# One 64-partition product in place of two 128-partition products when a norm's roots are spread to all partitions

## The chip, the cores and the metric

The kernel runs on one core of one Trainium2 chip. The metric is the device time of one execution in microseconds (us), the median of several runs. The engines of the core are named as the profile names them: PE (TensorE, products) with PEld (its weight loads), DVE (VectorE), ACT (ScalarE), POOL (GpSimd) and SP (SyncE, which issues most transfers). SBUF is the on-chip memory of 128 partitions, PSUM the memory that TensorE writes.

## The reference

A two-layer decoder trunk on one sequence of 512 tokens with 1024 features. What matters here is that each block begins with an RMSNorm, so that a root of a mean square over the features is wanted for every token, and that the product with the weights comes after it:

```python
def rmsnorm(x, g):
    xf = x.astype(jnp.float32)
    y = xf * lax.rsqrt(jnp.mean(xf * xf, axis=-1, keepdims=True) + EPS)
    return (y * g.astype(jnp.float32)).astype(x.dtype)
...
    for i in range(DEPTH):
        xn = rmsnorm(h, norm_mix[i])
        if i < N_A_LAYERS:
            a = i
            h = h + mixer_a(xn, a_w_in[a], a_norm_v[a], a_w_s[a], a_b_s[a], a_w_out[a])
        else:
            b = i - N_A_LAYERS
            h = h + mixer_b(xn, b_w_q[b], b_sinks[b], b_w_o[b], kblk, vblk)
        h = h + conv_ffn(rmsnorm(h, norm_ffn[i]), f_w_up[i], f_conv_w[i], f_conv_b[i], f_w_down[i])
        h = h + per_layer_embed(h, p[i], norm_ple[i], ple_w_in[i], ple_w_gate[i], ple_b_gate[i])
        if i == N_A_LAYERS - 1:
            kblk, vblk = shared_kv(h, norm_kv, w_kv)
    return rmsnorm(h, norm_final)
```

## The kernel before

**Layout.** The residual stream `h` lies with features on partitions: 8 tiles of 128 features x 512 tokens. Every weight is read once, in pieces of up to 1 MB (`load`, issued on SP in a fixed order), and cut into a high and a low half in the reduced type fp32r: `pump` copies the raw piece to `wh` on ScalarE (L163) and subtracts to get `wl` on VectorE (L164), one unit of 128 x 1024 at a time, with four units ahead of the one being multiplied. The activations are split likewise, and `mm3` (L190 to L192) or `mm3t` (L201 to L203) form a product as high x high + low x high + high x low.

**The norm.** Because the root is one number per token, it is not needed before the product with the weights: the product of the unnormalized, gain-scaled `h` is formed, and its result is multiplied by the root of each token. `Norm` does this. `take` or `square` squares each tile of `h` and adds the squares up in `acc` (128 x 512). `turn` transposes `acc` in blocks of 32 x 32 on VectorE and reduces each block, which leaves `quarter`: on 128 partitions, 16 numbers each. `begin` multiplies `quarter` by `alike`, which is four 128 x 32 blocks of stacked identities over D: the result `ps` (128 x 16 in PSUM) has the mean square of token 32 b + t on partition 32 a + t in column b, the same for each a from 0 to 3. `inv_root` then adds EPS on VectorE (L329) and raises to -1/2 on POOL (L331).

Before the change `begin` picks the columns so that `rt` is 128 x 4: token 128 c + p on partition p in column c (four small operations on VectorE, one for each quarter of the partitions). `rstd` turns it into a 128 x 512 tile, in which every partition holds the roots of all 512 tokens along the free axis: `spread` splits `rt` into `rh` and `rl`, multiplies the identity by each (two operations of 128 x 512 on VectorE, L344), sums over the partitions by two products with a 128 x 128 tile of ones (L347), and ScalarE copies the result out of PSUM (L320).

**Who uses which.** There are six norms of this class. In program order: n0 (ahead of the first mixer), nf0 (ahead of the first feed-forward block), np0 (first per-layer embedding), n1 (the shared keys and values, and the queries), nf1 and np1 (the same blocks in the second layer). In `ffn` (nf0, nf1) and `ple` (np0) `begin` stands behind the first 24 products of a chunk and `rstd` behind the next 24. Only `rstd` is used there. In n0, n1 and np1 the row form `rt` is used as well, where tokens lie on partitions: as the scale of the Gelu of n0 (L558), for the values of n1 (L711, L712 and `nrt`, L685), and for the last two blocks of 128 tokens in np1 (L998, L1001).

For n0, `begin` stands behind the products of the first half of the second column block of the mixer's `v` branch; 48 products follow ahead of `rstd`. ScalarE then goes through Gelu and squares of all eight `v` tiles, which ends in `sv` and a second root `vrt`; VectorE multiplies `zv` by it (L567), and PE reads `zv` in the products `s` (L584) behind the 48 products of the first chunk of `u`. For n1, `begin` stands behind the key products and `rstd` behind 24 query products. For np1, `begin` stands ahead of the last 24 products of 256 columns of the first four gate tiles, and eight transposes of `h` (L945) follow before `rstd`.

**Order.** The order of instructions on each engine is decided by a scheduler from program order, priorities and data; each engine then works through its own list in that order. An instruction that waits holds everything behind it on its engine.

Of the kernel before, what the change touches and what calls it, by code (L numbers as in the profile page):

```python
# [8 lines left out]
F32 = mybir.dt.float32  # L9
F32R = mybir.dt.float32r  # L10
AF = mybir.ActivationFunctionType
ALU = mybir.AluOpType

P = 128
D = 1024
S = 512
KD = D // P
NC = S // P
# [30 lines left out]
def tile_yoco(ctx: ExitStack, tc: tile.TileContext, t, out: bass.AP, out_b: bass.AP):  # L49
    nc = tc.nc  # L50

    const = ctx.enter_context(tc.tile_pool(name="const", bufs=1))
# [8 lines left out]
    def psum(name):  # L61
        return mmp.tile([P, S], F32, tag="mm", name=name)
# [178 lines left out]
                         start=True, stop=True)  # L241
    mean = const.tile([P, 1], F32, name="mean")
    nc.vector.memset(mean, 1.0 / D)
    minus_half = const.tile([P, NC], F32, name="minus_half")
    nc.vector.memset(minus_half, -0.5)
    ident = const.tile([P, P], F32, name="ident")
    make_identity(nc, ident)
# [2 lines left out]
    for q in range(4):  # L250
        s = slice(32 * q, 32 * (q + 1))
        nc.vector.tensor_scalar_mul(alike[s], ident[s, s].rearrange("p (o t) -> p o t", o=1).to_broadcast([32, 4, 32]),
                                    1.0 / D)


    def split_scaled(src, g, hi, lo):
# [15 lines left out]
    class Norm:  # L272
# [30 lines left out]
            nc.vector.tensor_reduce(self.quarter, sq.rearrange("p (b f) -> p b f", f=32),  # L303
                                    axis=mybir.AxisListType.X, op=ALU.add)

        def begin(self):

            if self.quarter is None:
                self.turn()
            ps = psum(f"{self.name}ms")[:, : S // 32]  # L310
            nc.tensor.matmul(ps, alike.rearrange("p a b -> p (a b)"), self.quarter, start=True, stop=True)
            ms = ps.rearrange("p (c r) -> p r c", r=4)
            self.rt = inv_root([(slice(32 * r, 32 * (r + 1)), ms[32 * r : 32 * (r + 1), r, :]) for r in range(4)],
                               self.name, n=NC)
            return self.rt

        def rstd(self):

            r = tp.tile([P, S], F32, tag="rstd", name=f"{self.name}rstd")
            nc.scalar.copy(r, spread(self.rt, NC, self.name))  # L320
            return r

    def inv_root(ms, name, scale=1.0, n=None):
        if n is None:
            n = ms.shape[1]
            ms = [(slice(None), ms)]
        m = const.tile([P, n], F32, tag=f"ms{n}", bufs=2, name=f"{name}m")
        for some, x in ms:
            nc.vector.tensor_scalar(m[some, :], x, scale, EPS, op0=ALU.mult, op1=ALU.add)  # L329
        r = const.tile([P, n], F32, tag=f"rt{n}", bufs=2, name=f"{name}rt")  # L330
        nc.gpsimd.tensor_tensor(r, m, minus_half[:, :n], op=ALU.pow)  # L331
        return r

    def spread(r, n, name):

        dh = tp.tile([P, n, P], F32R, tag="acc", name=f"{name}dh")
        dl = tp.tile([P, n, P], F32R, tag="acc", name=f"{name}dl")
        ps = psum(f"{name}sp")[:, : n * P]
        rh = const.tile([P, n], F32R, tag=f"rh{n}", bufs=1, name=f"{name}rh")
        nc.vector.tensor_copy(rh, r)  # L340
        rl = const.tile([P, n], F32, tag=f"rl{n}", bufs=1, name=f"{name}rl")
        nc.vector.tensor_sub(rl, r, rh.bitcast(F32))
        for d, x in ((dh, rh.bitcast(F32)), (dl, rl)):
            nc.vector.tensor_mul(d, ident.rearrange("p (o t) -> p o t", o=1).to_broadcast([P, n, P]),  # L344
                                 x.rearrange("p (c o) -> p c o", o=1).to_broadcast([P, n, P]))
        for d, st, en in ((dh, True, False), (dl, False, True)):
            nc.tensor.matmul(ps, ones, d.rearrange("p a b -> p (a b)"), start=st, stop=en)  # L347
        return ps
# [19 lines left out]
    def ffn(l, norm, nxt):  # L368

        xs = norm.xs[0][0]  # L370
        rstds = []

        def up(j):
            parts = chunk(256, KD)
            pss, cs = [], []
            for s in range(2):
                ps = psum(f"up{j}_{s}")
                mm3(ps, parts, xs, s * P)
                pss.append(ps)
                if j == 0:  # L380
                    rstds.append((norm.begin, norm.rstd)[s]())
            for s, ps in enumerate(pss):
                hs = tp.tile([P, S], F32, tag="hs", name=f"hs{j}_{s}")
                nc.vector.tensor_mul(hs, ps, rstds[1])  # L384
                col = s * NJ + j
                cw = [v("conv_w", (l * 3 + i) * 2 * NJ + col) for i in range(3)]
                c = tp.tile([P, S], F32, tag=f"c{s}", name=f"c{j}_{s}")
                nc.scalar.activation(c, hs, AF.Identity, bias=v("conv_b", l * 2 * NJ + col), scale=cw[2])  # L388
                nc.vector.scalar_tensor_tensor(c[:, 1:], hs[:, : S - 1], cw[1], c[:, 1:], op0=ALU.mult, op1=ALU.add)  # L389
                nc.vector.scalar_tensor_tensor(c[:, 2:], hs[:, : S - 2], cw[0], c[:, 2:], op0=ALU.mult, op1=ALU.add)  # L390
                cs.append(c)
            a = tp.tile([P, S], F32, tag="sg", name=f"a{j}")
            nc.scalar.activation(a, cs[0], AF.Silu)
            nc.vector.tensor_mul(a, a, cs[1])  # L394
            hi = ap.tile([P, S], F32R, tag=f"ah{j % SLOTS}", name=f"ah{j}")
            lo = ap.tile([P, S], F32R, tag=f"al{j % SLOTS}", name=f"al{j}")
            split(a, hi, lo)
            return hi, lo

        act = [up(0)]  # L400
        pe = None
        for i, (j0, j1) in enumerate(PARTS):
            act += [up(j) for j in range(j0 + 1, j1)]
            last = j1 == NJ
            if last:
                pe = ple_in_both() if l else ple_in(l)
            nact = [] if last else [up(j1)]
            dense_add(act, j1 - j0, nxt if last else None)
            act = nact
        return pe  # L410
# [44 lines left out]
    def ple(l, norm, nxt, pe):  # L455
        xs = norm.xs[0][0]
        rstd, held = None, []
        for c in range(4):
            parts = chunk(256, KD)
            for j in range(2):  # L460
                ps = psum(f"gate{c}_{j}")
                mm3(ps, parts, xs, j * P)
                held.append((2 * c + j, ps))
                if c == 0:
                    rstd = (norm.begin, norm.rstd)[j]()
                if c or j:
                    for m, ps in held:
                        z = tp.tile([P, S], F32, tag="hs", name=f"z{m}")
                        nc.vector.tensor_mul(z, ps, rstd)
                        sg = tp.tile([P, S], F32, tag="sg", name=f"gs{m}")  # L470
                        nc.scalar.activation(sg, z, AF.Sigmoid, bias=v("ple_b_gate", l * KD + m))
                        nc.vector.tensor_mul(sg, sg, pe[m])
                        nc.vector.tensor_add(h[m], h[m], sg)
                        nxt.take(m)
                    held = []
# [645 lines left out]
```

## Time and profile before

| | us |
|---|---|
| median of 3 runs | 1136.89 (1136.75 to 1136.90) |
| the profiled execution | 1136.71 |
| its span on the core | 1134.8 |
| PE busy | 1125.2 |
| DVE busy | 756.0 |
| ACT busy | 517.1 |
| POOL busy | 103.6 |

Rows of the timeline begin with the start in us from the start of the span and the duration in us; then come engine, line of the kernel, operation, output <- inputs, shapes and how many were merged. In square brackets stands how long the engine was idle before, and what ended that. A product's row on PE is longer than the time until the next one starts, because products are pipelined. Rows of groups end with the busy sum, the mean of one in ns, and the idle time ahead of the group with what ended it.

### The profile page before, as it was taken

What the parts mean: (1) busy time and instruction counts of PE and PEld (TensorE: products, weight loads), DVE (VectorE), ACT (ScalarE), POOL (GpSimd) and SP (SyncE); (2) the same over time, 40 slices, a digit from 0 to 9 for tenths busy, and PEclk for the clock granted to TensorE, in tenths of its full rate; (3) what the DMA queues carried; (4) which work ended last, traced back from release to release, by engine and by line L of the source; (5) the groups of instructions that cost most, each with busy time, mean ns of one, the idle gap of its engine ahead of it and who ended that gap; (6) DMA issues with size and microseconds to landing.
All of it is one profiled execution on the core that took longest, in us unless ns stands there. A gap on an engine that the chain in (4) does not pass through costs nothing.

```text
span 1134.8 us, 13579 instructions
## 1 busy us (share of the span) xinstructions
PE 1125.2 (99%) x5266; PEld 940.6 (83%) x5266; DVE 756.0 (67%) x1166; ACT 517.1 (46%) x827; POOL 103.6 (9%) x169
## 2 busy tenths in 40 slices
PE   9999999999999999999999999999999999999997
PEld 7888888888888888888888887888888888888896
DVE  7366477763677357557888997777636763675675
ACT  6533444441344234544656775444323442445562
POOL 2000200000000000021204451000000000000212
PEclk9999999999999999999999999999999999999999
DMA  8422323223232322333124323323223233224302
GB/s 300 140 88 75 111 75 111 86 100 112 75 102 92 101 95 89 109 105 107 69 81 130 82 87 126 135 75 111 94 92 111 66 102 111 93 88 154 112 1 75
DMA packets 25775, 115.40 MB, mean 102 GB/s; under 512 B 2920, under 2 KB 8176, under 8 KB 16240
## 3 DMA queue, kind: packets, MB, share of 16 engines
q1 hardware_dynamic: 25152, 113.89, 29.9%
q8 instruction: 41, 0.67, 0.3%
q10 hardware_dynamic: 560, 0.66, 0.2%
q14 instruction: 22, 0.18, 0.1%
HBM read 108.24 MB, written 2.11 MB: 97 GB/s over the span
## 4 chain that ended last, share of the span: by engine, by line
PE 94%; DVE 3%; issue 1%; DMA 1%; ACT 0%; POOL 0%; SPq 0%; POOLq 0%; DVEq 0%
PE up L190 14%; PE up L191 14%; PE up L192 14%; PE d L192 8%; PE d L190 8%; PE d L191 8%; PE gate L190 2%; PE gate L191 2%; PE gate L192 2%; PE u L191 1%; PE u L190 1%; PE u L192 1%; PE o L191 1%; PE o L192 1%; PE o L190 1%
## 5 line engine op out<-in xcount | busy, mean ns | idle before, releaser
L163 ACT CAST wh<-wraw 128x1024 fp32r<-128x1024 f32 (+2 forms) x197 | 202.0, 1028 | 265.0 <-PE d L191 131.3
L164 DVE TENSOR_TENSOR wl<-wraw,wh 128x1024 fp32r<-128x1024 f32 (+1 forms) x198 | 239.1, 1209 | 122.0 <-ACT wh L163 121.6
L190 PE MATMUL up<-nf00h,wh 128*128 128x512 f32 x352 | 137.1, 390 | 0.0
L190 PE MATMUL up<-nf10h,wh 128*128 128x512 f32 x352 | 137.0, 389 | 0.0
L191 PE MATMUL up<-nf00l,wh 128*128 128x512 f32 x352 | 136.9, 389 | 0.0
L192 PE MATMUL up<-nf00h,wl 128*128 128x512 f32 x352 | 136.9, 389 | 0.0
L191 PE MATMUL up<-nf10l,wh 128*128 128x512 f32 x352 | 136.9, 389 | 0.0
L192 PE MATMUL up<-nf10h,wl 128*128 128x512 f32 x352 | 136.9, 389 | 0.0
L190 PE MATMUL d<-ah,wh 128*128 128x512 f32 x352 | 136.9, 389 | 0.0
L191 PE MATMUL d<-al,wh 128*128 128x512 f32 x352 | 136.9, 389 | 0.0
L192 PE MATMUL d<-ah,wl 128*128 128x512 f32 x352 | 136.9, 389 | 0.0
L388 ACT ACTIVATE c<-hs,vec 128x512 f32<-128x512 f32 x88 | 71.5, 815 | 72.0 <-DVE hs L384 71.2
L389 DVE SCALAR_TENSOR_TENSOR c<-hs,vec,c 128x511 f32<-128x511 f32 x88 | 65.8, 749 | 34.5 <-ACT c L388 34.4
L364 DVE TENSOR_TENSOR h<-h,d 128x512 f32<-128x512 f32 x56 | 38.4, 686 | 74.0 <-PE d L192 74.0
L190 PEld LDWEIGHTS up<-nf00h,wh 128*128 128x128 f32 x352 | 66.1, 188 | 13.8
L191 PEld LDWEIGHTS up<-nf10l,wh 128*128 128x128 f32 x352 | 66.1, 188 | 13.8
L191 PEld LDWEIGHTS d<-al,wh 128*128 128x128 f32 x352 | 66.1, 188 | 13.7
L190 PEld LDWEIGHTS d<-ah,wh 128*128 128x128 f32 x352 | 66.1, 188 | 13.8
L192 PEld LDWEIGHTS up<-nf10h,wl 128*128 128x128 f32 x352 | 66.1, 188 | 13.7
L192 PEld LDWEIGHTS d<-ah,wl 128*128 128x128 f32 x352 | 66.1, 188 | 13.7
L192 PEld LDWEIGHTS up<-nf00h,wl 128*128 128x128 f32 x352 | 66.1, 188 | 13.7
L261 ACT CAST ah<-a 128x512 fp32r<-128x512 f32 x44 | 27.4, 622 | 109.7 <-DVE a L394 109.6
(453 smaller groups left out, 2050.1 us busy)
## 6 DMA issues: line engine op xcount, KB each, us to landing
wraw<-in_w_up SPq DMA_DIRECT2D x44, 1024.0 KB, 4.8
wraw<-in_w_down SPq DMA_DIRECT2D x16, 896.0 KB, 4.6
wraw<-in_w_down SPq DMA_DIRECT2D x8, 1024.0 KB, 4.9
wraw<-in_w_gate SPq DMA_DIRECT2D x8, 1024.0 KB, 4.8
wraw<-in_w_u SPq DMA_DIRECT2D x4, 1024.0 KB, 6.3
wraw<-in_w_out SPq DMA_DIRECT2D x4, 1024.0 KB, 4.8
wraw<-in_w_q SPq DMA_DIRECT2D x4, 1024.0 KB, 5.0
wraw<-in_w_o SPq DMA_DIRECT2D x4, 1024.0 KB, 4.9
```

The costliest lines, as they stand in the source:

```text
L163: nc.scalar.copy(hi, src)
L164: nc.vector.tensor_sub(low, src, hi.bitcast(F32))
L190: nc.tensor.matmul(ps, wh[:, a:b], xh, start=st, stop=False)
L191: nc.tensor.matmul(ps, wh[:, a:b], xl, start=False, stop=False)
L192: nc.tensor.matmul(ps, wl[:, a:b], xh, start=False, stop=en)
L261: nc.scalar.copy(hi, src)
L364: nc.vector.tensor_add(h[m], h[m], ps)
L388: nc.scalar.activation(c, hs, AF.Identity, bias=v("conv_b", l * 2 * NJ + col), scale=cw[2])
L389: nc.vector.scalar_tensor_tensor(c[:, 1:], hs[:, : S - 1], cw[1], c[:, 1:], op0=ALU.mult, op1=ALU.add)
```

## The change

`begin` now takes the mean squares of all 512 tokens from the first 64 partitions of `ps` as they lie there (64 x 16, so each token twice), and forms the root of all of them in one go on POOL. On all 64 partitions it rounds them to fp32r into `hl`; on partitions 32 to 63 it overwrites that with what the rounding lost. `rstd` multiplies `pick`, two stacked 32 x 32 identities, by `hl` (one operation of 64 x 512 on VectorE) and sums over the 64 partitions by one product with 64 rows of ones: the high halves on 32 of the partitions and the low halves on the others add up in the product itself. The row form `rt` is made as before, behind it, and only where it is used (`rows`); `ffn` and `ple` ask for none. `spread` stays for the final norm.

```diff
-    minus_half = const.tile([P, NC], F32, name="minus_half")
+    minus_half = const.tile([P, S // 32], F32, name="minus_half")
...
+    pick = const.tile([64, 32], F32, name="pick")
+    for q in range(2):
+        s = slice(32 * q, 32 * (q + 1))
+        nc.vector.tensor_copy(pick[s], ident[s, s])
...
-        def begin(self):
+        def begin(self, rows=True):
...
-            ps = psum(f"{self.name}ms")[:, : S // 32]
+            n = S // 32
+            ps = psum(f"{self.name}ms")[:, :n]
             nc.tensor.matmul(ps, alike.rearrange("p a b -> p (a b)"), self.quarter, start=True, stop=True)
-            ms = ps.rearrange("p (c r) -> p r c", r=4)
-            self.rt = inv_root([(slice(32 * r, 32 * (r + 1)), ms[32 * r : 32 * (r + 1), r, :]) for r in range(4)],
-                               self.name, n=NC)
-            return self.rt
+            r = inv_root([(slice(None), ps[:64])], f"{self.name}s", n=n, parts=64)
+
+            self.hl = const.tile([64, n], F32R, tag="hl", bufs=1, name=f"{self.name}hl")
+            nc.vector.tensor_copy(self.hl, r)
+            low = slice(32, 64)
+            nc.vector.tensor_sub(self.hl[low], r[low], self.hl[low].bitcast(F32))
+            if rows:
+                ms = ps.rearrange("p (c r) -> p r c", r=4)
+                self.rt = inv_root([(slice(32 * r, 32 * (r + 1)), ms[32 * r : 32 * (r + 1), r, :]) for r in range(4)],
+                                   self.name, n=NC)
+                return self.rt
...
+            n = S // 32
+            d = tp.tile([64, n, 32], F32R, tag="acc", name=f"{self.name}d")
+            nc.vector.tensor_mul(d, pick.rearrange("p (o t) -> p o t", o=1).to_broadcast([64, n, 32]),
+                                 self.hl.bitcast(F32).rearrange("p (c o) -> p c o", o=1).to_broadcast([64, n, 32]))
+            ps = psum(f"{self.name}sp")
+            nc.tensor.matmul(ps, ones[:64], d.rearrange("p a b -> p (a b)"), start=True, stop=True)
             r = tp.tile([P, S], F32, tag="rstd", name=f"{self.name}rstd")
-            nc.scalar.copy(r, spread(self.rt, NC, self.name))
+            nc.scalar.copy(r, ps)
...
-    def inv_root(ms, name, scale=1.0, n=None):
+    def inv_root(ms, name, scale=1.0, n=None, parts=P):
...
-                    rstds.append((norm.begin, norm.rstd)[s]())
+                    rstds.append(norm.rstd() if s else norm.begin(rows=False))
...
-                    rstd = (norm.begin, norm.rstd)[j]()
+                    rstd = norm.rstd() if j else norm.begin(rows=False)
```

In the order that the scheduler gives to VectorE, the instructions of a norm with rows are: the wide addition of EPS, two of the four narrow ones, the rounding copy (which waits for POOL), a narrow one, the subtraction, a narrow one, then `d`; at n1 a weight split (L164) stands ahead of `d`, and at n0 one stands behind it. `nrt` comes behind `d`. The two copies of `pick` stand right behind the four of `alike`. PE's order is the same but for the product that is gone; on ScalarE and VectorE the order of a few neighbours differs in both feed-forward blocks and in np0's block.

More of the change, by code (lines that the diff above doesn't have):

```diff
@@ L326, in inv_root @@
             ms = [(slice(None), ms)]
-        m = const.tile([P, n], F32, tag=f"ms{n}", bufs=2, name=f"{name}m")
+        m = const.tile([parts, n], F32, tag=f"ms{n}", bufs=1 if parts < P else 2, name=f"{name}m")
         for some, x in ms:
             nc.vector.tensor_scalar(m[some, :], x, scale, EPS, op0=ALU.mult, op1=ALU.add)
-        r = const.tile([P, n], F32, tag=f"rt{n}", bufs=2, name=f"{name}rt")
-        nc.gpsimd.tensor_tensor(r, m, minus_half[:, :n], op=ALU.pow)
+        r = const.tile([parts, n], F32, tag=f"rt{n}", bufs=1 if parts < P else 2, name=f"{name}rt")
+        nc.gpsimd.tensor_tensor(r, m, minus_half[:parts, :n], op=ALU.pow)
         return r
```

## The prediction

> **What bounds the kernel now.** I read the page first: its busy shares and its chain of waits.
>
> ```profile
> span 1134.8 us, 13579 instructions
> PE 1125.2 (99%) x5266; PEld 940.6 (83%) x5266; DVE 756.0 (67%) x1166; ACT 517.1 (46%) x827; POOL 103.6 (9%) x169
> PE 94%; DVE 3%; issue 1%; DMA 1%; ACT 0%; POOL 0%; SPq 0%; POOLq 0%; DVEq 0%
> ```
>
> TensorE is busy for 99% and carries 94% of the chain, so a product taken away is worth its spacing, and whatever makes PE wait costs its full length. The view of waits, for PE alone, says how rare that is today:
>
> ```profile
> PE o L191 <- POOL ol L867: 0.8, 1, 0.8
> PE v L203 <- DVE wl L164: 0.4, 1, 0.4
> ```
>
> None of the six norms makes PE wait for its root now. So the question at each is whether the new way of making `d` still ends before PE reaches the spread product, and what a second root behind it delays.
>
> **The products removed.** Each norm's two spread products become one. The timeline of PE at nf0 (columns here and below: start and duration in us):
>
> ```profile
> 156.46 0.40 PE L347 MATMUL nf0sp<-nf0dh,ones 128*128 128x512 f32 x1
> 156.69 0.39 PE L347 MATMUL nf0sp<-nf0dl,ones 128*128 128x512 f32 x1
> 156.93 0.39 PE L190 MATMUL up<-nf00h,wh 128*128 128x512 f32 x1
> ```
>
> Starts are 0.23 us apart though a row lasts 0.39. Half the partitions do not shorten the streaming of 512 columns, so one product is saved, not one and a half: 6 x 0.23 = -1.38 us.
>
> **A product on 64 rows.** No row shows one. The only shape other than 128\*128 in the trace is the 128\*8 pair:
>
> ```profile
> 145.09 0.38 PE L605 MATMUL turned<-ident,vec 128*8 128x128 f32 x2
> ...
> 145.54 0.40 PE L191 MATMUL up<-nf00l,wh 128*128 128x512 f32 x1
> ```
>
> From 145.09 to 145.54 stream 2 x 128 + 512 columns, 1.5 times 0.23 = 0.34 us at the usual pace; 0.11 more were spent. I take 0.11 for each change of shape and back, since that is the nearest row: 6 x 0.11 = +0.66. Below, it is 0. Above, both ends of the odd product lie bare: a row lasts 0.39 and the next starts after 0.23, so 0.16 of tail is hidden, twice that is 0.32; and if weight loads can't run ahead either, 0.19 more each:
>
> ```profile
> L190 PEld LDWEIGHTS up<-nf00h,wh 128*128 128x128 f32 x352 | 66.1, 188 | 13.8
> ```
>
> so 0.70 a norm, 4.2 in all. The Trainium skill, TensorEngine Tiling (Array Packing), section Tiling Modes, says that a change of the tiling mode, 64 rows against 128 among them, drains the array; by it the sum would hold the two bare tails instead of my 0.11. That is rival B. No run here shows it yet.
>
> **The root on POOL.** It grows from 128x4 to 64x16, so from 4 elements a partition to 16. Groups of POOL by shape:
>
> ```profile
> L331 POOL TENSOR_TENSOR n1rt<-n1m,minus_half 128x4 f32<-128x4 f32 x1 | 1.0, 1018 | 10.5 <-DVE n1m L329 10.5
> L331 POOL TENSOR_TENSOR fin0rt<-fin0m,minus_half 128x2 f32<-128x2 f32 x1 | 0.7, 708 | 1.5 <-DVE fin0m L329 1.5
> L331 POOL TENSOR_TENSOR fin1rt<-fin1m,minus_half 128x1 f32<-128x1 f32 x1 | 0.5, 547 | 0.0
> ```
>
> 1, 2 and 4 columns take 547, 708 and 1018 ns: 155 to 161 a column. Sixteen: 1018 + 12 x 155 = 2878 ns, 1.86 more than now. Partitions need not help, as they work side by side. Below: 1.02, if width were free; above: four times 1.02, 4.07. I take 2.88, as three rows lie on one line.
>
> **Norms without rows (nf0, np0, nf1).**
>
> ```profile
> 151.09 0.67 DVE L329 TENSOR_SCALAR nf0m<-nf0ms 32x4 f32<-32x4 f32 x4 [0.93 <-PE nf0ms L311]
> ...
> 153.78 0.68 DVE L344 TENSOR_TENSOR nf0dl<-ident,nf0rl 128x512 fp32r<-128x512 f32 x1
> ```
>
> One tensor_scalar (0.67 / 4, about 0.16) stands for four, then 0.08 until POOL starts, 2.88, 0.04 back, two small operations (about 0.4 with their dependence) and one multiplication of 0.68: `d` is ready at 151.09 + 4.25 = 155.3. PE needs it at 156.46, so 1.1 us are to spare and PE's own 24 products hide it. DVE stands still during the root, but the weight split behind it is read by PE four units later. The same sum leaves 1.1 at np0 and nf1. Cost: none.
>
> **np1.** Here `begin` also makes row roots, and only 24 products of 256 columns and 8 transposes cover it:
>
> ```profile
> 1087.97 0.67 DVE L329 TENSOR_SCALAR np1m<-np1ms 32x4 f32<-32x4 f32 x4 [1.36 <-PE np1ms L311]
> 1089.78 0.17 DVE L340 CAST np1rh<-np1rt 128x4 fp32r<-128x4 f32 x1 [1.13 <-POOL np1rt L331]
> 1090.66 0.68 DVE L344 TENSOR_TENSOR np1dl<-ident,np1rl 128x512 fp32r<-128x512 f32 x1
> 1088.72 1.02 POOL L331 TENSOR_TENSOR np1rt<-np1m,minus_half 128x4 f32<-128x4 f32 x1 [10.38 <-DVE np1m L329]
> 1091.53 0.47 PE L347 MATMUL np1sp<-np1dh,ones 128*128 128x512 f32 x1
> ```
>
> (1088.72 - 1087.97 - 0.67 is the 0.08 used above; 1089.78 - 1088.72 - 1.02 the 0.04.) `dl` ends at 1091.34, only 0.19 before PE comes. In the new order of DVE, the wide tensor_scalar and two of the four narrow ones come first, then the copy that waits for POOL, a narrow one, the subtraction, a narrow one, `d`. So `d` runs from 1087.97 + 3.6 = 1091.57 to 1092.25 and PE starts at 1092.28: a stall of 0.75 us. Everything after it follows the gate products, so it stays: +0.75.
>
> **n1.** The same order, with a weight split now ahead of `d`:
>
> ```profile
> 572.30 0.66 DVE L329 TENSOR_SCALAR n1m<-n1ms 32x4 f32<-32x4 f32 x4
> 574.25 1.22 DVE L164 TENSOR_TENSOR wl<-wraw,wh 128x1024 fp32r<-128x1024 f32 x1
> 576.06 0.68 DVE L344 TENSOR_TENSOR n1dl<-ident,n1rl 128x512 fp32r<-128x512 f32 x1
> 577.10 0.40 PE L347 MATMUL n1sp<-n1dh,ones 128*128 128x512 f32 x1
> ```
>
> Before, that split filled DVE's time behind the root. Now it starts at 572.30 + 3.6 = 575.9, holds DVE for some 1.15, and `d` ends at 577.73: PE starts at 577.77 instead of 577.10, +0.67.
>
> **n0.** PE reaches the spread product 11 us after `begin`, so `d` is early. But the row roots feed ScalarE's Gelu, and they come last:
>
> ```profile
> 40.32 1.04 POOL L331 TENSOR_TENSOR n0rt<-n0m,minus_half 128x4 f32<-128x4 f32 x1 [12.11 <-DVE n0m L329]
> 41.57 0.72 ACT L558 ACTIVATE zv<-zv,n0rt 128x512 f32<-128x512 f32 x1
> 41.57:53.90 12.33, 12.26 (x27) 1.00 0.26 87
> 55.42 2.74 DVE L567 TENSOR_SCALAR zv<-zv,vrt 128x1024 f32<-128x1024 f32 x4 [1.13 <-POOL vrt L331]
> 61.73 1.95 PE L584 MATMUL s<-wsT,zv 128*128 128x128 f32 x16
> ```
>
> The third row is ScalarE alone: busy 12.26 of 12.33 us, so a late root moves its whole run, and `zv`, which now ends at 58.16. The second root's input is ready near 43.3, but `d` (two SBUF inputs) has started by then and the split behind it follows without a gap. POOL and such an operation exclude each other in this trace:
>
> ```profile
> 1077.04 1.30 POOL L291 TENSOR_TENSOR np1acc<-np1acc,np1sq 128x512 f32<-128x512 f32 x1 [2.87 <-ACT np1sq L286]
> 1077.44 1.45 DVE L164 TENSOR_TENSOR own_al<-wraw,own_ah 128x512 fp32r<-128x512 f32 x1 [0.28 <-ACT own_ah L163]
> 600.52 0.69 DVE L817 TENSOR_TENSOR prs<-prs,ds 128x512 f32<-128x512 f32 x1
> 601.12 1.22 DVE L164 TENSOR_TENSOR wl<-wraw,wh 128x1024 fp32r<-128x1024 f32 x1
> 600.67 1.77 POOL L698 CAST diff<-vd 128x64 fp32r<-128x64 f32 x1 [0.41 <-DVE vd L719]
> L698 POOL CAST diff<-vd x12: 230/236/1767, 590.9 to 603.6; 128x64 fp32r<-128x64 f32 x12
> ```
>
> The split took 1.45 where 128x512 takes 0.68, and a cast of 0.24 took 1.77, through two operations of DVE. So the second root runs from 45.0 to 46.0, Gelu starts 4.48 later and `zv` ends at 62.64. PE comes to the fourth `s` product at 61.73 - 0.23 + 0.11 + 3 x 0.11 = 61.94: a stall of 0.7. If POOL gets in first, `zv` ends near 61.1 and it is 0; with a root of 4.07 it is 1.9. In n1 and np1 the second root has time: its first readers, `nrt` and `zt`, stand at or behind the spread product.
>
> **The start.** `pick` adds two 32x32 copies to DVE right after `alike`, in a stretch where DVE is full:
>
> ```profile
> 11.12 0.91 DVE L252 TENSOR_SCALAR alike<-ident 32x128 f32<-32x128 f32 x4
> 11.00:23.00 12.00, 11.81 (x51) 9.12 (x49) 11.65 (x20) 9.96 (x15) 0.00 (x0) 1.00 0.96 339
> ```
>
> (columns: PE, PEld, DVE, ACT, POOL: DVE 11.65 of 12 us), and at its end PE waits for the split (the 0.4 above), so it is paid in full. `alike` takes 0.23 apiece at four times the width: 0.1 each, +0.2 (0.1 to 0.45). The wider memset is 12 elements more; nothing.
>
> **The sum.** -1.38 + 0.66 + 0.75 + 0.67 + 0.7 + 0.2 = +1.60 on the profiled execution's 1136.71: 1138.3. Its median is 1136.89, so the two bases differ by 0.18. A change under 0.2% (2.3 us) I call none.
>
> **The rivals.**
> B, slower: the array drains around the 64-row product. Two tails of 0.16, at all six norms: 6 x 0.32 = 1.9 in place of 0.66, so 1139.6; with bare weight loads 4.2, so 1141.8. It passes the 0.2% from 0.22 us a norm on ((2.27 - 0.94) / 6, 0.94 being the sum without this term). For it: 0.16 of every product is hidden now. Against: 128\*8 cost 0.11.
> C: the root's width is nearly free. `d` is in time everywhere, and only the products count: -1.38 + 0.66 + 0.2 = -0.5, 1136.2. Against: 547, 708, 1018.
> D, slower: the root takes 4.07. The three stalls grow by 1.19 each and the covered norms begin to wait, 0.15 each: 1.6 + 3.6 + 0.45, 1142.3.
> That TensorE is no longer the limit I don't count: it idles under 1% now.
>
> **How the numbers follow.** Forecast 0.45, B 0.25, C 0.16, D 0.14. The forecast's and C's times lie within 0.2%; slower are D, most of B and 0.05 of the forecast: 0.38. The saving is at most 1.4 us, so faster is 0.02, and 0.60 is left. The range runs from C's time to the dearer B, 1136.0 to 1141.6.
>
> **What would show it.** Roots of 64x16 near 2.88 us on POOL; at np1 and n1 a wait of PE for `d` of 0.7; the second root of n0 starting only when the weight split ends, and PE waiting for `zv`; the gap from the spread product's start to the next product near 0.3 us and from the product before it near 0.23. I am wrong if the roots are short, if the gaps around the spread product exceed 0.5, or if PE waits at nf0, np0 or nf1.

## The result, and the profile after

The changed kernel took 1140.06 us (median of 9 runs, 1139.62 to 1140.42) against 1136.89 (9 runs, 1136.64 to 1137.11): 3.17 us more, ratio 1.0029 with a 95% interval of 1.0018 to 1.0039. So it is slower, by the medians by 0.28%; the interval's lower end, 0.18%, lies just under the 0.2% that the prediction calls a change. The time lies inside the range given. The likeliest case, a change within 0.2%, did not come about. Its profiled execution took 1139.62 us.

The page of after, with the rows that answer to those of before: the span, the busy times and the chain.

```profile
span 1137.9 us, 13559 instructions
...
PE 1126.6 (99%) x5260; PEld 939.2 (83%) x5260; DVE 751.9 (66%) x1156; ACT 516.8 (45%) x827; POOL 121.1 (11%) x172
...
PE 90%; DVE 5%; ACT 2%; issue 1%; POOL 1%; DMA 0%; SPq 0%; POOLq 0%; DVEq 0%; ACTq 0%
```

Six products are gone from PE (5266 to 5260) and DVE works 4.1 us less. The span is 3.1 us longer all the same, and DVE, ACT and POOL now hold 8% of the chain, where they had 3%. The view of waits, for PE (who waits, for whom; us in total, times, the longest), names the places:

```profile
PE np1sp L339 <- DVE np1d L336: 0.9, 1, 0.9
...
PE n1sp L339 <- DVE n1d L336: 0.6, 1, 0.6
...
PE s L605 <- DVE zv L588: 0.2, 1, 0.2
```

These three waits are new, and no wait stands at nf0, np0 or nf1. They sum to 1.7 us. Six products saved ought to pay 1.4 of that, so something costs that isn't a wait. The timeline of PE at nf0 shows it:

```profile
156.85 0.39 PE L192 MATMUL up<-nf00h,wl 128*128 128x512 f32 x1
157.17 0.49 PE L339 MATMUL nf0sp<-nf0d,ones 64*128 64x512 f32 x1
157.59 0.50 PE L190 MATMUL up<-nf00h,wh 128*128 128x512 f32 x1
157.93 0.40 PE L191 MATMUL up<-nf00l,wh 128*128 128x512 f32 x1
```

The three starts behind the first row follow after 0.32, 0.42 and 0.34 us. Three ordinary steps are 0.69, these are 1.08. No row has a bracket, so nothing was late here: the product on 64 rows is itself the cause, or stands beside it.

To compare kernels without the start, which moves from one profile to the next, I subtract starts of the same PE rows. Each cell is the start of the second row named minus that of the first, in us. "ms" is the sum over partitions in `begin`, "sp" the (first) spread product, s the first of the products that read `zv`.

| from, to | before | after | after - before |
|---|---|---|---|
| n0ms, n0sp | 11.13 | 11.22 | +0.09 |
| n0sp, s | 11.36 | 11.48 | +0.12 |
| s, nf0ms | 89.04 | 89.51 | +0.47 |
| nf0ms, nf0sp | 5.69 | 5.78 | +0.09 |
| nf0sp, np0ms | 365.20 | 365.32 | +0.12 |
| np0ms, np0sp | 5.69 | 5.78 | +0.09 |
| np0sp, n1ms | 44.00 | 44.11 | +0.11 |
| n1ms, n1sp | 5.75 | 6.50 | +0.75 |
| n1sp, nf1ms | 136.37 | 136.38 | +0.01 |
| nf1ms, nf1sp | 5.68 | 5.79 | +0.11 |
| nf1sp, np1ms | 368.49 | 368.61 | +0.12 |
| np1ms, np1sp | 3.89 | 5.03 | +1.14 |
| np1sp, fin0sp | 24.31 | 24.27 | -0.04 |
| all, n0ms to fin0sp | 1076.60 | 1079.78 | +3.18 |

Each norm without a stall loses 0.2 us although a product is gone. The two norms with a late `d` lose 0.76 and 1.10, and the late `zv` 0.47. Four norms with 0.21, 0.21, 0.20 and 0.23, and these three, are the 3.18.

At np1, DVE's timeline, with the spread product of PE under it:

```profile
1089.99 0.17 DVE L350 TENSOR_SCALAR np1sm<-np1ms 64x16 f32<-64x16 f32 x1 [1.35 <-PE np1ms L319]
...
1093.17 0.17 DVE L323 CAST np1hl<-np1srt 64x16 fp32r<-64x16 f32 x1 [2.79 <-POOL np1srt L352]
1093.37 0.16 DVE L350 TENSOR_SCALAR np1m<-np1ms 32x4 f32<-32x4 f32 x1
1093.56 0.16 DVE L325 TENSOR_TENSOR np1hl<-np1srt,np1hl 32x16 fp32r<-32x16 f32 x1
1093.76 0.17 DVE L350 TENSOR_SCALAR np1m<-np1ms 32x4 f32<-32x4 f32 x1
1093.96 0.68 DVE L336 TENSOR_TENSOR np1d<-pick,np1hl 64x512 fp32r<-64x512 f32 x1
1094.69 0.50 PE L339 MATMUL np1sp<-np1d,ones 64*128 64x512 f32 x1 [0.91 <-DVE np1d L336]
```

The bracket on the second row is the wide root: DVE stands still for 2.79 us. Then four small operations, 0.20 apart, come before `d`, which begins 3.97 us after the first row. The roots of POOL, grouped by shape (busy us, mean ns, idle before):

```profile
L352 POOL TENSOR_TENSOR np1srt<-np1sm,minus_half 64x16 f32<-64x16 f32 x1 | 2.9, 2908 | 9.9 <-DVE np1sm L350 9.9
...
L352 POOL TENSOR_TENSOR n0rt<-n0m,minus_half 128x4 f32<-128x4 f32 x1 | 2.7, 2683 | 0.9 <-DVE n0m L350 0.9
...
L352 POOL TENSOR_TENSOR vrt<-vm,minus_half 128x4 f32<-128x4 f32 x1 | 1.0, 1017 | 12.8 <-DVE vm L350 12.8
```

The wide root takes 2.91. The narrow one at n0 takes 2.68, while the same shape alone takes 1.02. What that does at n0 is seen in the timeline of POOL, DVE, ACT and PE:

```profile
43.55 2.68 POOL L352 TENSOR_TENSOR n0rt<-n0m,minus_half 128x4 f32<-128x4 f32 x1 [0.87 <-DVE n0m L350]
43.51 0.69 DVE L336 TENSOR_TENSOR n0d<-pick,n0hl 64x512 fp32r<-64x512 f32 x1
44.12 1.21 DVE L164 TENSOR_TENSOR wl<-wraw,wh 128x1024 fp32r<-128x1024 f32 x1
...
46.27 0.72 ACT L579 ACTIVATE zv<-zv,n0rt 128x512 f32<-128x512 f32 x1 [4.78 <-POOL n0rt L352]
...
60.12 2.74 DVE L588 TENSOR_SCALAR zv<-zv,vrt 128x1024 f32<-128x1024 f32 x4 [1.13 <-POOL vrt L352]
...
61.88 0.86 PE L605 MATMUL s<-wsT,zv 128*128 128x128 f32 x6
...
64.05 0.48 PE L190 MATMUL u<-n00h,wh 128*128 128x512 f32 x1
```

The root ends at 46.23, 0.90 after the split of DVE (44.12 + 1.21 = 45.33). The Gelus start 4.70 later than before, `zv` is complete at 62.86, and the `s` products begin at 61.88 and stop for the last of it.

### The profile page after: what moved, and what is told of

It reads as the page before. It is cut to its first block, busy times and chain, and to the rows that moved or that the text cites. A ratio compares the mean times of both kernels' runs of the same rounds, so it can differ in the third digit from the quotient of the medians.

```text
span 1137.9 us, 13559 instructions
## 1 busy us (share of the span) xinstructions
PE 1126.6 (99%) x5260; PEld 939.2 (83%) x5260; DVE 751.9 (66%) x1156; ACT 516.8 (45%) x827; POOL 121.1 (11%) x172
## 4 chain that ended last, share of the span: by engine, by line
PE 90%; DVE 5%; ACT 2%; issue 1%; POOL 1%; DMA 0%; SPq 0%; POOLq 0%; DVEq 0%; ACTq 0%
PE up L190 14%; PE up L191 14%; PE up L192 14%; PE d L190 8%; PE d L191 8%; PE d L192 8%; PE gate L190 2%; PE gate L192 2%; PE gate L191 2%; PE o L191 1%; PE o L192 1%; PE o L190 1%; PE u L191 1%; PE u L192 1%; PE u L190 1%
## 5 line engine op out<-in xcount | busy, mean ns | idle before, releaser
L164 DVE TENSOR_TENSOR wl<-wraw,wh 128x1024 fp32r<-128x1024 f32 (+1 forms) x198 | 238.8, 1207 | 122.4 <-ACT wh L163 121.8
L190 PEld LDWEIGHTS up<-nf10h,wh 128*128 128x128 f32 x352 | 66.1, 188 | 13.9 <-issue 0.2
L191 PEld LDWEIGHTS up<-nf00l,wh 128*128 128x128 f32 x352 | 66.1, 188 | 13.6
```

Of the source, the lines that this page charges most:

```text
L164: nc.vector.tensor_sub(low, src, hi.bitcast(F32))
L190: nc.tensor.matmul(ps, wh[:, a:b], xh, start=st, stop=False)
L191: nc.tensor.matmul(ps, wh[:, a:b], xl, start=False, stop=False)
```

## The experiments

The theory after the result: the 64-row product costs more than it saves, and the rest is three late inputs. Times are medians of 5 to 11 runs, always beside runs of before on the same chip (1136.80 to 1136.87).

| kernel | us | ratio to before, 95% |
|---|---|---|
| e1, one product over 128 rows | 1137.93 | 1.0010 (1.0001 to 1.0018) |
| e2, 64-row product twice | 1141.66 | 1.0043 (1.0030 to 1.0057) |
| e3, at n0 the narrow root first | 1139.85 | 1.0026 (1.0015 to 1.0036) |
| e4, n1 and np1 as before | 1138.51 | 1.0014 (1.0006 to 1.0023) |
| e5, one product over 96 rows | 1138.75 | 1.0015 (1.0007 to 1.0024) |
| e6, diagonal early at n1 and np1 | 1139.51 | 1.0024 (1.0015 to 1.0033) |
| e7, the useful parts, 4 norms | 1136.44 | 0.9995 (0.9987 to 1.0004) |
| e8, the useful parts, 5 norms | 1136.07 | 0.9993 (0.9984 to 1.0002) |
| e9, before with the selector alone | 1137.12 | 1.0003 (0.9994 to 1.0011) |
| e10, e8 with the selector on GpSimd | 1135.76 | 0.9990 (0.9981 to 0.9999) |
| e11, before again | 1136.94 | 1.0000 (0.9991 to 1.0008) |

The stretches that tell them apart, made as in the table above:

| from, to | before | after | e1 | e2 | e3 | e4 | e5 | e6 | e8 | e10 |
|---|---|---|---|---|---|---|---|---|---|---|
| nf0ms, nf0sp | 5.69 | 5.78 | 5.70 | 5.78 | 5.79 | 5.77 | 5.70 | 5.78 | 5.69 | 5.69 |
| nf0sp, np0ms | 365.20 | 365.32 | 364.95 | 365.51 | 365.31 | 365.30 | 364.98 | 365.32 | 365.02 | 365.02 |
| s, nf0ms | 89.04 | 89.51 | 89.03 | 89.34 | 89.03 | 89.57 | 89.96 | 89.54 | 89.04 | 89.04 |
| n1ms, n1sp | 5.75 | 6.50 | 6.52 | 6.79 | 6.51 | 5.69 | 6.50 | 5.78 | 5.69 | 5.69 |
| n1sp, nf1ms | 136.37 | 136.38 | 136.24 | 136.57 | 136.39 | 136.39 | 136.17 | 136.43 | 136.13 | 136.10 |
| np1ms, np1sp | 3.89 | 5.03 | 5.07 | 5.04 | 5.05 | 3.88 | 5.06 | 5.04 | 3.87 | 3.87 |
| n0ms to fin0sp | 1076.60 | 1079.78 | 1077.27 | 1081.09 | 1079.33 | 1077.86 | 1078.21 | 1079.19 | 1075.66 | 1075.59 |

### e1: the same product, 128 rows

```diff
-    pick = const.tile([64, 32], F32, name="pick")
+    pick = const.tile([P, 32], F32, name="pick")
+    nc.gpsimd.memset(pick, 0.0)
...
-            r = inv_root([(slice(None), ps[:64])], f"{self.name}s", n=n, parts=64)
+            r = inv_root([(slice(None), ps)], f"{self.name}s", n=n, parts=P)
...
-            d = tp.tile([64, n, 32], F32R, tag="acc", name=f"{self.name}d")
+            d = tp.tile([P, n, 32], F32R, tag="acc", name=f"{self.name}d")
...
-            nc.tensor.matmul(ps, ones[:64], d.rearrange("p a b -> p (a b)"), start=True, stop=True)
+            nc.tensor.matmul(ps, ones, d.rearrange("p a b -> p (a b)"), start=True, stop=True)
```

(`hl` and the multiplication that makes `d` have 128 partitions likewise; the last 64 of the selector are zero.)

> Kernel after, with the one spread product of each norm over 128 partitions: the selector, the wide root and the diagonal have 128 partitions, with zeros in the selector below the first 64, so that the product adds zeros and has the same shape of rows as every product beside it. Theory (a product over 64 rows between products over 128 costs about 0.4 us a norm in the two steps around it): at nf0 the three steps from the last product before the spread to the second one after it fall from 1.08 us to about 0.69, six norms give 6 x 0.39 = 2.3 us back, 1140.06 becomes about 1137.7, 0.8 us over the kernel before. Rival (the time goes with the lone product whatever its rows are: its diagonal, its place among the others, the copy behind it): the steps stay 1.08 us and the time stays 1140.

Measured 1137.93. PE's timeline of this kernel at nf0:

```profile
156.35 0.40 PE L192 MATMUL up<-nf00h,wl 128*128 128x512 f32 x1
156.59 0.39 PE L340 MATMUL nf0sp<-nf0d,ones 128*128 128x512 f32 x1
156.82 0.39 PE L190 MATMUL up<-nf00h,wh 128*128 128x512 f32 x1
```

Steps of 0.24 and 0.23: with zeros for the missing rows the price is gone. Against after, the way into the product falls by 0.08 and the stretch behind it by 0.37, so the shape cost 0.45 us at nf0. The three steps alone (1.08 against 0.69) hold 0.39 of that. The other 0.06 come in the next 3 us, and e8, which has the same product at nf0, doesn't win them back (5.69 into it and 365.02 behind it), so 0.39 to 0.45 is as near as the runs put it.

The weight loads show where the time goes. PEld's timeline at nf0, of after and then of e1:

```profile
157.17 0.18 PEld L339 LDWEIGHTS nf0sp<-nf0d,ones 64*128 64x128 f32 x1 [0.35 <-DVE wl L164]
157.59 0.19 PEld L190 LDWEIGHTS up<-nf00h,wh 128*128 128x128 f32 x1 [0.24 <-issue]
```

```profile
156.36 0.19 PEld L340 LDWEIGHTS nf0sp<-nf0d,ones 128*128 128x128 f32 x1
156.59 0.19 PEld L190 LDWEIGHTS up<-nf00h,wh 128*128 128x128 f32 x1
```

In e1 each load starts 0.23 us ahead of its product (156.59 and 156.82) and runs under the one before. In after both loads start together with their products (157.17 and 157.59): across the change of shape no load ran ahead. Whether the array also empties first, these rows don't separate. The wait on `wl` that the first bracket names is not the cause: in e1 the same load starts 0.30 before that split ends.

At n1 only 0.14 - 0.02 comes back: where PE stood still anyway, much of the price was covered. Of the 2.51 us less between n0ms and fin0sp, 0.48 are not the shape: the wait for `zv` was gone too, since in this profile the narrow root at n0 took 1.52 us instead of 2.68. That leaves 2.03 for the shape.

### e2: the product twice

```diff
-            nc.tensor.matmul(ps, ones[:64], d.rearrange("p a b -> p (a b)"), start=True, stop=True)
+            for _ in range(2):
+                nc.tensor.matmul(ps, ones[:64], d.rearrange("p a b -> p (a b)"), start=True, stop=True)
```

> Kernel after, with the 64-row product of each norm issued twice in a row (the second writes the same result over the first, nothing else changes). If the price lies in the change of shape on the way in and out, the second product follows the first within an ordinary 0.23 us and six of them cost 1.4 us: 1141.5. If each 64-row product pays for itself (about 0.23 + 0.39), they cost 3.7 us: 1143.8; if the drain is hidden partly (0.49 us per product, the duration of its row), about 2.9 us: 1143.0.

Measured 1141.66, 1.60 over after. PE's timeline of this kernel at nf0 (the second row merges both products):

```profile
157.15 0.39 PE L192 MATMUL up<-nf00h,wl 128*128 128x512 f32 x1
157.46 0.73 PE L340 MATMUL nf0sp<-nf0d,ones 64*128 64x512 f32 x2
158.12 0.50 PE L190 MATMUL up<-nf00h,wh 128*128 128x512 f32 x1
158.46 0.40 PE L191 MATMUL up<-nf00l,wh 128*128 128x512 f32 x1
```

From the first of the two to the next 128-row product pass 0.66 us, with one it was 0.42: the second costs 0.24, an ordinary step. In is 0.31 and out 0.34, as with one. So the price is paid for the change of shape, once in and once out, not for each product on 64 rows. (The way into the spread of n1 is 0.29 longer here than in after, in a stretch where PE waits for `d`. VectorE's wide addition starts there 0.96 behind n1ms (573.06 to 574.02) and 0.67 in after (572.38 to 573.05), as a weight split holds VectorE until then; before the change it was 0.95.)

### e5: 96 rows

```diff
-            r = inv_root([(slice(None), ps[:64])], f"{self.name}s", n=n, parts=64)
+            r = inv_root([(slice(None), ps[:96])], f"{self.name}s", n=n, parts=96)
...
-            nc.tensor.matmul(ps, ones[:64], d.rearrange("p a b -> p (a b)"), start=True, stop=True)
+            nc.tensor.matmul(ps, ones[:96], d.rearrange("p a b -> p (a b)"), start=True, stop=True)
```

(The selector, `hl` and `d` have 96 partitions likewise, the last 32 of the selector zero.)

> As the kernel with 128 padded partitions, but with 96: the selector holds zeros on 32 partitions below the 64 used ones. Theory (the array knows row shapes of a few sizes, and a product over 96 rows runs in the same one as 128): steps at nf0 of about 0.23 us, time as with 128 rows, 1137.9. Rival (any product over fewer rows than its neighbours pays, by the count of its rows): at nf0 the step into it is 0.3 us and the two out of it 0.34 each or half of that extra, time 1139 to 1140.

PE's timeline of this kernel at nf0:

```profile
157.81 0.40 PE L192 MATMUL up<-nf00h,wl 128*128 128x512 f32 x1
158.05 0.40 PE L340 MATMUL nf0sp<-nf0d,ones 96*128 96x512 f32 x1
158.28 0.40 PE L190 MATMUL up<-nf00h,wh 128*128 128x512 f32 x1
```

Steps of 0.24 and 0.23, and the stretches around nf0 are e1's (5.70; 364.98 against 364.95). The time, 1138.75, is 0.8 over the expected 1137.9, and the stretches show where: 0.93 from s to nf0ms, in which the wait for `zv` is back (the narrow root took 2.68 again). It is longer than in after (0.47) because PE, with the shape's price gone, comes there 0.42 earlier (22.28 from n0ms to s, against 22.70). At the spread nothing is lost. So fewer rows alone don't cost: 64 do and 96 don't.

The Trainium skill, TensorEngine Tiling (Array Packing), section Tiling Modes, lists row tilings of 128, 64 and 32 rows and says that a change of mode drains the engine. The three runs agree, as far as prices go: 0.39 to 0.45 us for a visit to 64 rows, an ordinary step for a second product there, nothing for 96, which is no mode in that list. The draining itself no row shows.

### e3: the Gelus of n0

```diff
+            def by_row():
+                ms = ps.rearrange("p (c r) -> p r c", r=4)
+                self.rt = inv_root([(slice(32 * r, 32 * (r + 1)), ms[32 * r : 32 * (r + 1), r, :]) for r in range(4)],
+                                   self.name, n=NC)
+            if rows and self.name == "n0":
+                by_row()
             r = inv_root([(slice(None), ps[:64])], f"{self.name}s", n=n, parts=64)
...
             if rows:
-                ms = ps.rearrange("p (c r) -> p r c", r=4)
...
+                if self.name != "n0":
+                    by_row()
```

> Kernel after, but in the norm n0 alone the root of four columns, which the Gelus wait for, is made ahead of the wide root of sixteen. Theory (the Gelus start 4.7 us late, zv ends late and the s products wait 0.2 us and run 0.5 us behind): Gelus start near 43 us, the wait of s on zv is gone, the offset of 0.53 us that appears between 51 and 63 us is gone: 1139.5. Rival (that offset is not the Gelus' lateness but the order of products there): Gelus early, the offset stays, 1140.0.

Measured 1139.85, 0.2 under after, with intervals that overlap: the time alone decides nothing. ACT's timeline of this kernel does:

```profile
43.21 0.72 ACT L585 ACTIVATE zv<-zv,n0rt 128x512 f32<-128x512 f32 x1 [0.95 <-POOL n0rt L358]
```

The first Gelu waits 0.95 us for the root instead of 4.78, PE's wait for `zv` is gone from the view of waits, and the stretch from s to nf0ms is 89.03, as before the change. So the wait for `zv` costs 0.48 us, and the order of the two roots makes it.

### e4: n1 and np1 as before

```diff
+            if self.name in OLD:
+                ms = ps.rearrange("p (c r) -> p r c", r=4)
+                self.rt = inv_root([(slice(32 * r, 32 * (r + 1)), ms[32 * r : 32 * (r + 1), r, :]) for r in range(4)],
+                                   self.name, n=NC)
+                return self.rt
...
+            if self.name in OLD:
+                r = tp.tile([P, S], F32, tag="rstd", name=f"{self.name}rstd")
+                nc.scalar.copy(r, spread(self.rt, NC, self.name))
+                return r
```

with `OLD = ('n1', 'np1')`.

> Kernel after, but in the norms n1 and np1 alone the path of the kernel before (only the root of four columns, split into halves of 128 partitions, two products). Theory (there the spread waits for the wide root, 0.6 and 0.9 us of waits in the trace, offsets of 0.9 and 1.1 us gained across the two spreads): both waits are gone, the gain is 0.9 + 1.1 = 2.0 us, 1138.1; the four other norms keep 4 x 0.15 us for the shape and 0.53 us for the Gelus, 1.1 us over the kernel before. Rival (the offsets at these two are mostly the 64-row product, the same price at all six norms, and the waits are only where it shows): the gain is 2 x 0.4 = 0.8 us at most, 1139.3.

Measured 1138.51, 1.55 under after; the stretches give 1079.78 - 1077.86 = 1.92. The ways into the two spreads are 5.69 and 3.88 (5.75 and 3.89 before the change), and PE's only wait for a norm's work left is the 0.2 for `zv`. The rival allowed 0.8 at most. It falls: at these two norms it is mainly the late `d` that costs, and the shape only the 0.12 and 0.13 that e1 gives back there.

### e6: the diagonal before what was put ahead of it

```diff
+            if self.name in ("n1", "np1"):
+                self.diagonal()
             if rows:
...
         def rstd(self):
...
-            d = tp.tile([64, n, 32], F32R, tag="acc", name=f"{self.name}d")
-            nc.vector.tensor_mul(d, pick.rearrange("p (o t) -> p o t", o=1).to_broadcast([64, n, 32]),
-                                 self.hl.bitcast(F32).rearrange("p (c o) -> p c o", o=1).to_broadcast([64, n, 32]))
+            if self.name not in ("n1", "np1"):
+                self.diagonal()
+            d = self.d
```

(`diagonal` is the multiplication taken out here.)

> Kernel after, but at n1 and np1 alone VectorE multiplies the diagonal right behind the halves of the wide root, ahead of the last small operations for the root of four columns and, at n1, ahead of the 1.23 us split of a weight. Theory (the diagonal is late by what stands between the halves and it on VectorE): at n1 it ends near 577.4 us, the wait is gone, and the 6.50 us from the norm's sum to the spread falls to the 5.78 us of the other norms while the 0.35 us behind the spread show; at np1 it comes 0.4 us earlier (two small operations of 0.2), 5.03 falls to 4.6 us; in all 0.7 + 0.4 - 0.2 = 0.9 us, 1139.2. Rival (the wide root itself is the whole lateness, and what is moved back is late in its turn, the split at n1 and the second root): the same stall shows behind the spread, 1140.0.

DVE's timeline of this kernel at n1 and at np1:

```profile
577.92 0.17 DVE L358 TENSOR_SCALAR n1m<-n1ms 32x4 f32<-32x4 f32 x1
578.12 0.68 DVE L337 TENSOR_TENSOR n1d<-pick,n1hl 64x512 fp32r<-64x512 f32 x1
578.73 1.21 DVE L164 TENSOR_TENSOR wl<-wraw,wh 128x1024 fp32r<-128x1024 f32 x1
...
1094.25 0.17 DVE L358 TENSOR_SCALAR np1m<-np1ms 32x4 f32<-32x4 f32 x1
1094.45 0.68 DVE L337 TENSOR_TENSOR np1d<-pick,np1hl 64x512 fp32r<-64x512 f32 x1
```

At n1 `d` now stands ahead of the split: the way into the spread falls from 6.50 to 5.78, the wait is gone, and the split came back later at no loss (136.43 behind). The lateness at n1 was the split, as the prediction had it. The small operations stayed where they were, because the scheduler kept them ahead of `d` at both norms. So half of this experiment did not happen, and np1 is unchanged at 5.04. The time, 1139.51, is 0.55 under after and the stretches give 0.59.

### e7, e8 and e10: what the change is good for

e7 takes one 128-row product at n0 (narrow root first), nf0, np0 and nf1, and the two products of before at n1 and np1. e8 takes the one product at n1 as well, with `d` early. e10 is e8 with

```diff
-        nc.vector.tensor_copy(pick[s], ident[s, s])
+        nc.gpsimd.tensor_copy(pick[s], ident[s, s])
```

> A version meant to keep what the change saves: one product over 128 padded partitions at n0 (with the root of four columns made first), nf0, np0 and nf1, and the path of the kernel before, two products, at n1 and np1. Theory: against the kernel before one product of 0.23 us less at four norms and no stall, 0.9 us faster: 1135.9; none of the waits on a diagonal or on zv is left. Rival (the saved products are given back elsewhere, at the start by the selector or behind the later copies): 1136.8, no difference.

> As the version with 128 padded partitions at n0, nf0, np0 and nf1, but n1 too takes the one padded product, with its diagonal made ahead of the small operations and the split of a weight; np1 alone keeps two products. Theory (diagonal ready near 577.4 us, before the spread is due): 0.23 us more saved, 1135.7. Rival (the split moved back by 0.7 us is late for the products behind it, or the root of four columns is late for its reader): no gain over the version with two products at n1, or 0.5 us lost, 1136.4.

> The version with one padded product at n0, nf0, np0, nf1 and n1 and two products at np1, with the two copies of the selector on GpSimd instead of VectorE. Theory (the copies cost 0.36 us at the start): the step from alike to the split behind it on VectorE is 0.94 us again, the time 0.3 to 0.4 us under that version's 1136.07: 1135.7. Rival (they cost nothing there, or GpSimd's copies hold VectorE up as much): 1136.1.

e7 came to 1136.44 and e8 to 1136.07, each a little over what was expected and neither told apart from before by its interval. In the stretches most of the saved products are there: 0.79 us for four norms in e7 (1076.60 - 1075.81) and 0.94 for five in e8, 0.19 to 0.20 each where 0.23 was expected, and no wait on a norm is left. e10 took 1135.76, 1.06 under before with an interval just clear of 1, and the slowest of its 11 runs (1136.08) lies under the fastest of the 27 of before beside it (1136.21). It is the fastest kernel here. That is 0.1%, below the 0.2% that I call a change.

### e9 and e11: the start

e9 adds to before only these lines, whose result nothing reads; e11 is before unchanged.

```diff
+    pick = const.tile([64, 32], F32, name="pick")
+    for q in range(2):
+        s = slice(32 * q, 32 * (q + 1))
+        nc.vector.tensor_copy(pick[s], ident[s, s])
```

> Kernel before plus the two copies that make the selector of 64 partitions, whose result nothing reads. Theory (VectorE is busy without a gap from about 8 us to the weight split that TensorE waits for at 23.2 us, so the 0.36 us that the two copies take between alike and the next split come out at that wait): the step from the start of alike to the split behind it is 1.30 us in place of 0.94, and the time is 0.36 us above before: 1137.2. Rival (a transfer, not VectorE, sets the first wait): no difference, 1136.9.

> Kernel before, unchanged, as one of the kernels compared: how far two sets of runs of one kernel differ, and how far the first wait of TensorE moves from one profile to the next. Expected 1136.9, ratio 1.000 within 0.0005; the wait near 23 us ending within 0.8 us of the 23.23 of the profile of before, its later parts, from the n0 sum to the last spread, 1076.60 us as there.

DVE's timeline of e9, then that of e10:

```profile
11.20 0.91 DVE L252 TENSOR_SCALAR alike<-ident 32x128 f32<-32x128 f32 x4
12.12 0.35 DVE L258 COPY pick<-ident 32x32 f32<-32x32 f32 x2
12.51 0.75 DVE L263 SCALAR_TENSOR_TENSOR n00l<-h,vec,n00h 128x512 fp32r<-128x512 f32 x1
```

```profile
11.47 0.90 DVE L252 TENSOR_SCALAR alike<-ident 32x128 f32<-32x128 f32 x4
12.41 0.76 DVE L265 SCALAR_TENSOR_TENSOR n00l<-h,vec,n00h 128x512 fp32r<-128x512 f32 x1
```

From `alike` to the next split pass 1.31 us with the copies on VectorE and 0.94 without. The times fit 0.37 (e9 0.30 over before, e10 0.31 under e8, or 0.26 when each is set against the runs of before on its own chip), but e9's interval holds zero as well and e10's overlaps e8's, so the price at the end of the kernel isn't settled by them. Adding 0.37 to what the stretches differ from before brings most kernels near their medians (e1 0.67 + 0.37 = 1.04, measured 1.13; e2 4.86, measured 4.86; e4 1.63, measured 1.71; e7 -0.42, measured -0.43), but not after itself (3.55, measured 3.17) nor e6 (2.96, measured 2.64). e11 gave 1136.94 against 1136.82, and its stretch from n0ms to fin0sp is 1076.61 against 1076.60. The whole stretch repeats to hundredths of a microsecond, the part from n1sp to nf1ms to 0.03. The start doesn't: n0ms began at 39.24 in one profile of before and at 39.39 in the other, and anywhere from 39.18 to 40.26 in the others.

## Why the prediction was right and wrong

**The step that failed** is the term "A product on 64 rows": "I take 0.11 for each change of shape and back, since that is the nearest row: 6 x 0.11 = +0.66". The runs showed 0.45 us at a norm without a stall by e1, four times as much, and 0.12 and 0.13 at n1 and np1 (6.50 to 6.52 and 136.38 to 136.24; 5.03 to 5.07 and 24.27 to 24.10), where PE stood still anyway: 2.03 in all by e1. The nearest row was misread. It prices a product of 128 columns at a quarter of 0.23, but such products start 0.11 apart in the full shape too, as the prediction itself has it for the `s` products. PE's timeline of before, at the last two of these:

```profile
63.29 0.39 PE L584 MATMUL s<-wsT,zv 128*128 128x128 f32 x2
63.43 0.48 PE L190 MATMUL u<-n00h,wh 128*128 128x512 f32 x1
63.75 0.40 PE L191 MATMUL u<-n00l,wh 128*128 128x512 f32 x1
```

Two products of 128 columns and one of 512 take 0.46 here (63.29 to 63.75), all on 128\*128, and 0.45 with 128\*8. So the 0.11 goes with the short products, and that row held no price for a change of shape.

With 0.45, a norm turns from a gain of 0.23 into a loss of 0.2, and this alone carries the time over the 0.2% line. Rival B came nearer: e1, e2 and e5 show a price for the change itself, and the rows of PEld show the loads that can't run ahead, which its dearer case named (at 0.70 a norm, too much). That the array drains is argued, not shown. The price of 0.32 was low: the runs show 0.09 on the way in and 0.30 to 0.36 on the way out. That its 1139.6 lies near the measured 1140.06 is partly luck, since 0.32 at all six norms is too little at four and too much at n1 and np1, and the sums (1.92 and 2.03) come out alike. Its warning sign, gaps over 0.5, was set too wide: the gaps were 0.32, 0.42 and 0.34.

**The products removed**: right in kind. In e1 and e5, at nf0, one is worth 0.25 and 0.22 (365.20 against 364.95 and 364.98), in e8 0.18 (365.02), but at n1 only 0.13 (136.37 against 136.24 in e1), behind the stall. All six together come to 1.27 in e1, not 1.38.

**The root**: 2.88 forecast, 2.91 measured. Rivals C and D fall.

**Norms without rows**: no wait at nf0, np0, nf1, as forecast.

**np1**: a stall of 0.75 forecast, 1.14 measured. The reason is in the timeline: `d` begins 3.97 us behind the first row, not 3.6. My 3.6 left 0.44 for the four small operations behind the root (3.6 - 0.16 - 0.08 - 2.88 - 0.04); they stand 0.20 apart and took 0.79 (1093.96 - 1093.17). That is nearly the whole difference. e6 was to show it by moving them and didn't, so it rests on the rows alone.

**n1**: 0.67 forecast, 0.75 measured, with the split as the cause (e6).

**n0**: 0.7 forecast, 0.47 measured (e3), by the steps forecast: the second root blocked until the split ends, Gelu 4.70 later where 4.48 was said, `zv` at 62.86 where 62.64 was said. PE lost less than the end of `zv` suggests because the shape's price brings it to `s` 0.21 later than before (22.70 from n0ms, against 22.49), where the forecast had it 0.12 earlier. In e5, where it comes 0.21 earlier (22.28), the same late `zv` costs 0.93.

**The start**: 0.2 forecast. The copies take 0.37 of DVE's full stretch (e9, e10), inside the 0.1 to 0.45 given. The profile of after doesn't show it at PE's wait, because its `alike` began 0.42 earlier than in the profile of before.

The stretches sum to 3.18 where these terms without the start make 1.40. Of the 1.78 missing, 1.37 are the shape (2.03 - 0.66) and 0.39 np1. n1 gives 0.08 more and n0 0.23 less, and the products save 0.11 less. The 0.06 left are the ways into the spreads of n1 and np1, 0.02 and 0.04 longer in e1 than in after. The ends of the prediction's range, 1136.0 and 1141.6, lie 0.2 under the times that it works out for C and the dearer B, 1136.2 and 1141.8.

## What to carry to other kernels

Here a single product on 64 rows among products on 128 cost more (0.39 to 0.45 us) than a second product of the usual shape (0.23), so try filling the missing rows with zeros before you shrink a product. Such a price is read from the starts of the rows around it and of their weight loads, not from waits, since none is shown. A row taken as a price must be compared with a row that differs from it in that one thing alone. A wider operation on a slow engine is free only where something covers it: look at each place of use by itself, and keep the old form where cover is short. Where two results come from one engine, make the one first whose reader is on the longer chain.

## What the runs showed of the hardware

- A change from 128 to 64 rows and back costs 0.39 to 0.45 us, a second 64-row product beside the first only 0.24, and 96 rows nothing. Across the change the weight load starts with its product, not 0.23 us ahead of it.
- The same narrow root on POOL, behind the same two operations of DVE, took 2.68 us in after and e5, and 1.52 in e1. POOL's timeline at n0, e1 first and then e5:

```profile
44.00 1.52 POOL L353 TENSOR_TENSOR n0rt<-n0m,minus_half 128x4 f32<-128x4 f32 x1 [0.88 <-DVE n0m L351]
```

```profile
44.49 2.68 POOL L353 TENSOR_TENSOR n0rt<-n0m,minus_half 128x4 f32<-128x4 f32 x1 [0.87 <-DVE n0m L351]
```

In e1 it ended 0.26 us before DVE's split did (44.56 + 1.22 = 45.78), so it had not waited for the split; in e5 it ended 0.91 after it (45.05 + 1.21 = 46.26). The Trainium skill, SBUF — State Buffer, section SBUF: two separate sides, says that GpSimd and a VectorE operation with two SBUF inputs hold a shared pair of ports in turn, each for a whole instruction. The row of e5 agrees, as the root ended only behind the split. The row of e1 doesn't for GpSimd's side: the root ended 0.96 us into the split, which still took 1.22, against 1.21 in e5. The timeline of e8 at n0, POOL and DVE, shows the same:

```profile
41.15 1.04 POOL L376 TENSOR_TENSOR n0rt<-n0m,minus_half 128x4 f32<-128x4 f32 x1 [12.26 <-DVE n0m L374]
41.19 1.23 DVE L164 TENSOR_TENSOR wl<-wraw,wh 128x1024 fp32r<-128x1024 f32 x1
```

So a split holds this small root up, but a root that goes first lengthens the split by no more than 0.02. That the two exclude each other, as the prediction put it, holds for this pair in one order only. What decides who goes first no run here shows, and a wait for `zv` hangs on it that cost 0.47 in after and 0.93 in e5.
